# One extra load ahead of the position loads: 8 bytes from each of 111 stretches of the embedding table, read by every DMA engine

## The chip, the cores and the metric

The kernel runs on one core of one Trainium2 chip. The metric is device time in microseconds (us), the median of several executions. The text also uses the *span* of a profiled execution, from the first to the last instruction that the profile shows; in undisturbed runs here it is about 2 us shorter than the device time.

## The reference

```python
def setup_inputs():
    batch, seq_len, vocab_size, d_model = 32, 512, 50000, 512
    ...   # int32 indices, float32 table (50000 x 512), float32 positions (512 x 512)

def reference(indices, embedding_table, position_embed):
    token_embed = embedding_table[indices]
    return (token_embed + position_embed).astype(np.float32)
```

It looks up 16,384 rows of 2 KB each in a table of 102 MB, adds a position row to each, and writes 33.5 MB. The indices reach the chip as 64-bit integers.

## The kernel before

GpSimd issues 128 gathers. Each fetches 128 rows, one per partition (256 KB). VectorE adds the position rows, which ScalarE has copied to PSUM, and SyncE issues the stores: one per gather in the first two batches and the last, one per two gathers in five more, one per batch of four gathers (1 MB) in the rest. All small loads go out on SyncE's queue, in the order in which they are written.

```python
    idx0 = const.tile([P, 2 * K], i32)
    nc.sync.dma_start(out=idx0[:], in_=idx_first)               # indices of batch 0
    idx_raw = const.tile([B, S, 2], i32)
    nc.sync.dma_start(out=idx_raw[:], in_=idx_words.rearrange("b (s w) -> b s w", w=2))
    pos_sb = [const.tile([P, D], f32, name=f"pos_sb{k}") for k in range(K)]
    for k in range(K):
        nc.sync.dma_start(out=pos_sb[k][:], in_=pos_rows[:, k, :])
    ...                                                          # indices turned: idx_t
    pos_ps = [psum.tile([P, D], f32, name=f"pos_ps{k}") for k in range(K)]
    for k in range(K):
        nc.scalar.copy(out=pos_ps[k][:], in_=pos_sb[k][:])

    def chunk(b, parts):
        at = 0
        for n in parts:
            data = data_pool.tile([P, n, D], f32, tag="data")
            for j in range(n):
                k = at + j
                where = idx0[:, 2 * k : 2 * k + 1] if b == 0 else idx_t[:, k, b : b + 1]
                nc.gpsimd.indirect_dma_start(out=data[:, j, :], out_offset=None, in_=table,
                    in_offset=bass.IndirectOffsetOnAxis(ap=where, axis=0))
                nc.vector.tensor_tensor(out=data[:, j, :], in0=data[:, j, :],
                                        in1=pos_ps[k][:], op=add)
            nc.sync.dma_start(out=out_rows[b][:, at : at + n, :], in_=data[:])
            at += n
```

## Time and profile before

| | before |
|---|---|
| device time, median of 3 | 184.50 us (184.49 to 184.75) |
| the profiled execution | 177.94 us, span 176.2 us |
| moved by DMA | 68.33 MB |
| GpSimd, 128 gathers | 1.25 us from one to the next |

The profiled execution is 6.6 us shorter than the timed ones.

The first lines are from the page of the kernel before. "DMA" is the mean busy share, in tenths, of the core's 16 DMA engines in 40 equal slices of the span; "GB/s" is what they moved. The line with L88 is the group of gathers: busy time, mean ns of one, and the idle time before them. The last lines are DMA issues with the median us from issue to landing.

```profile
span 176.2 us, 480 instructions
DMA  4889999999999999999999999999999999999995
GB/s 131 305 236 354 384 380 387 414 410 406 417 378 397 413 413 407 402 404 390 419 419 415 415 421 412 415 413 414 419 420 416 415 408 421 406 399 406 413 411 205
...
DMA 57%; POOL 27%; issue 11%; DVE 2%; POOLq 0%; DVEq 0%
...
L88 POOL DMA_INDIRECT data<-in_embedding_table_dram,idx_t x124 | 117.2, 945 | 39.8 <-issue 33.7
...
data<-in_embedding_table_dram,idx_t POOLq DMA_INDIRECT x124, 7.7
pos_sb<-in_position_embed_dram SPq DMA_DIRECT2D x4, 256.0 KB, 4.7
```

From the seventh slice to the last but one the DMA engines move 378 to 421 GB/s and are busy throughout. In slices 2 and 3 (counted from 0; 9 to 18 us) they are busy too, and move less. That stretch is what the change was made for.

The timeline of GpSimd in the same trace shows the first gather, three in the middle, and the last. The columns are start, duration, engine, line, operation, and in brackets the idle time before.

```profile
2.94 1.14 POOL L88 DMA_INDIRECT data<-in_embedding_table_dram,idx  x1 [1.74 <-DMA idx<-in_indices_dram]
...
40.61 0.95 POOL L88 DMA_INDIRECT data<-in_embedding_table_dram,idx_t  x1 [0.30 <-issue]
41.86 0.95 POOL L88 DMA_INDIRECT data<-in_embedding_table_dram,idx_t  x1 [0.30 <-issue]
43.11 0.95 POOL L88 DMA_INDIRECT data<-in_embedding_table_dram,idx_t  x1 [0.30 <-issue]
...
163.88 0.95 POOL L88 DMA_INDIRECT data<-in_embedding_table_dram,idx_t  x1 [0.30 <-DVE data L94]
```

GpSimd takes one step of 1.25 us per gather. Had it kept that step from the first gather (2.94, which is followed by one gap of 1.44) to the end, the last gather would start at 2.94 + 1.44 + 126 x 1.25 = 161.9 us. It starts at 163.9. 256 KB per 1.25 us is 210 GB/s of reads and, in time, as much of writes. So GpSimd asks for 420 GB/s, and the DMA engines deliver 414 over the 60 us from 100 us on.

### The profile page before, as it was taken

To read this page: it belongs to the slowest core of one execution; us is meant where nothing else is said; L and a number is where in the kernel's file an instruction comes from. 1 tells how busy PE (TensorE), PEld (TensorE's weight loads), DVE (VectorE), ACT (ScalarE), POOL (GpSimd) and SP (SyncE) were. 2 spreads that over 40 slices of the span, in tenths; PEclk is the share of its full clock that TensorE was granted. 3 is DMA by queue.
4 is the path that set the end of the run, shared out by engine and by line. 5 is a ranking of instruction groups with operands and counts; after the bars stand their busy time and mean duration, and the time that the engine had idled before them with its cause. 6 is when DMAs were issued, how large, how long until landed. Compare 5 with 4: busy or idle time off the path is not lost.

```text
span 176.2 us, 480 instructions
## 1 busy us (share of the span) xinstructions
PE 0.7 (0%) x4; PEld 0.6 (0%) x4; DVE 87.7 (50%) x130; ACT 3.6 (2%) x5; POOL 121.7 (69%) x134
## 2 busy tenths in 40 slices
PE   0100000000000000000000000000000000000000
PEld 0100000000000000000000000000000000000000
DVE  1162554454744447354466464544647464444740
ACT  2410000000000000000000000000000000000000
POOL 3777777777777777777777777777777756777300
DMA  4889999999999999999999999999999999999995
GB/s 131 305 236 354 384 380 387 414 410 406 417 378 397 413 413 407 402 404 390 419 419 415 415 421 412 415 413 414 419 420 416 415 408 421 406 399 406 413 411 205
DMA packets 17635, 68.33 MB, mean 388 GB/s; under 512 B 3008, under 2 KB 3008, under 8 KB 14560
## 3 DMA queue, kind: packets, MB, share of 16 engines
q0 software_dynamic: 10240, 33.56, 50.2%
q1 hardware_dynamic: 7392, 34.74, 48.1%
q14 instruction: 3, 0.02, 0.0%
HBM read 34.74 MB, written 33.55 MB: 388 GB/s over the span
## 4 chain that ended last, share of the span: by engine, by line
DMA 57%; POOL 27%; issue 11%; DVE 2%; POOLq 0%; DVEq 0%
DMA data<-in_embedding_table_dram,idx_t 56%; POOL data L88 27%; DVE data L94 2%; DMA idx<-in_indices_dram 1%; POOLq L88 0%; DVEq L94 0%
## 5 line engine op out<-in xcount | busy, mean ns | idle before, releaser
L88 POOL DMA_INDIRECT data<-in_embedding_table_dram,idx_t x124 | 117.2, 945 | 39.8 <-issue 33.7
L94 DVE TENSOR_TENSOR data<-data,pos_ps 128x512 f32<-128x512 f32 x128 | 86.9, 687 | 79.6 <-DMA data<-in_embedding_table_dram,idx_t 72.7
L88 POOL DMA_INDIRECT data<-in_embedding_table_dram,idx x4 | 4.0, 993 | 2.7 <-DMA idx<-in_indices_dram 1.7
L79 ACT COPY pos_ps<-pos_sb 128x512 f32<-128x512 f32 x4 | 2.4, 589 | 4.9 <-DMA pos_sb<-in_position_embed_dram 4.8
L68 DVE CAST idx_f<-idx_raw 32x512 f32<-32x512 int32 x1 | 0.5, 523 | 3.8 <-DMA idx_raw<-in_indices_dram 3.8
L79 ACT ACT_TABLE_LOAD x1 | 1.3, 1283 | 0.8 <-PEq L121 0.8
L75 DVE CAST idx_t<-turned 128x128 int32<-128x128 f32 x1 | 0.3, 292 | 0.8 <-PE turned L73 0.8
L73 PE MATMUL turned<-ident,idx_f 32*128 32x32 f32 x4 | 0.7, 300 | 4.4 <-DVE idx_f L68 4.4
L73 PEld LDWEIGHTS turned<-ident,idx_f 32*128 32x128 f32 x4 | 0.6, 206 | 4.4 <-issue 4.4
L121 POOL MEMSET const-float32-0.0<- 128x1 f32 x1 | 0.1, 105 | 0.3 <-issue 0.3
L60 POOL MEMSET ones<- 32x32 f32 x1 | 0.1, 114 | 0.3 <-POOLq L121 0.3
L62 POOL TENSOR_SCALAR_AFFINE_SELECT ident<-ones 32x32 f32<-32x32 f32 x1 | 0.2, 202 | 0.1
L121 POOL MEMSET const-uint8-127<- 128x1 uint8 x1 | 0.1, 122 | 0.0
L121 POOL MEMSET const-bfloat16-1.0<- 128x1 bf16 x1 | 0.1, 116 | 0.0
L121 POOL MEMSET const-float32-1.0<- 128x1 f32 x1 | 0.1, 108 | 0.0
## 6 DMA issues: line engine op xcount, KB each, us to landing
out_dram<-data SPq DMA_DIRECT2D x24, 1024.0 KB, 7.7
out_dram<-data SPq DMA_DIRECT2D x10, 512.0 KB, 6.9
out_dram<-data SPq DMA_DIRECT2D x12, 256.0 KB, 5.8
data<-in_embedding_table_dram,idx_t POOLq DMA_INDIRECT x124, 7.7
pos_sb<-in_position_embed_dram SPq DMA_DIRECT2D x4, 256.0 KB, 4.7
idx_raw<-in_indices_dram SPq DMA_DIRECT2D x1, 128.0 KB, 2.5
data<-in_embedding_table_dram,idx POOLq DMA_INDIRECT x4, 4.7
idx<-in_indices_dram SPq DMA_DIRECT2D x1, 4.0 KB, 1.8
```

Source lines behind the costliest of these rows:

```text
L60: nc.gpsimd.memset(ones[:], 1.0)
L62: nc.gpsimd.affine_select(out=ident[:], in_=ones[:], pattern=[[-1, B]], compare_op=mybir.AluOpType.is_equal, fill=0.0, base=0, channel_mul ...
L68: nc.vector.tensor_copy(out=idx_f[:].rearrange("b p k -> b (p k)"), in_=idx_raw[:, :, 0])
L73: nc.tensor.transpose(turned[:, k, :], idx_f[:, :, k], ident[:])
L75: nc.vector.tensor_copy(out=idx_t[:], in_=turned[:])
L79: nc.scalar.copy(out=pos_ps[k][:], in_=pos_sb[k][:])
L88: nc.gpsimd.indirect_dma_start(out=data[:, j, :], out_offset=None, in_=table, in_offset=bass.IndirectOffsetOnAxis(ap=where, axis=0),)
L94: nc.vector.tensor_tensor(out=data[:, j, :], in0=data[:, j, :], in1=pos_ps[k][:], op=add)
L121: nc = _bacc.Bacc("TRN2", target_bir_lowering=False, num_devices=1)
```

## The change

The idea is that an engine's first read in some part of the table may be slow, and that 8 bytes read early from each part take that slowness out of the gathers. The load is third in SyncE's queue: behind the indices, which the gathers need at once, and ahead of the position rows.

```diff
+STRETCHES = 112
...
     nc.sync.dma_start(
         out=idx_raw[:], in_=idx_words.rearrange("b (s w) -> b s w", w=2)
+    )
+
+    step = -(-V // STRETCHES)
+    touched = const.tile([16, V // step, 2], f32)
+    nc.sync.dma_start(
+        out=touched[:],
+        in_=bass.AP(table.tensor, 0, [[0, 16], [step * D, V // step], [1, 2]]),
     )
     pos_sb = [const.tile([P, D], f32, name=f"pos_sb{k}") for k in range(K)]
```

`step` is 447 rows (0.92 MB), so there are 111 reads per engine. Nothing reads `touched`.

## The prediction

> **What bounds the kernel now.** The 16 DMA engines. From slice 6 of 40 on, the page's DMA row reads 9 tenths and the GB/s row 380 to 420; the kernel moves 68.33 MB, which at 415 GB/s alone takes 165 of the 176.2 us span. GpSimd issues one gather of 256 KB per 1.25 us, 210 GB/s of reads and as much of writes: 420 together, just what the DMA carries. So a backlog made early is never worked off: the issue loop alone would start the last gather at 161.7 us; it starts at 163.9 and lands 7.3 us later.
>
> **Where it loses time.** The GB/s row begins 131 305 236 354 384 380. From 9 to 18 us the engines are busy (8 tenths and more) and move little. The DMA records show why: a gather packet of 4096 B takes 159 ns in the steady state, but 230 to 440 ns on average from 9 to 13 us, single ones over 1000. Summed over the run, gather packets lose 6.0 us per engine against 159 ns, about half of it in the first 24 of 128 gathers. By 26.4 us 7.9 MB are moved; at 415 GB/s from the first store (9.3 us) it would be 9.3 MB. So 3 to 3.5 us are lost at the start. I take it that an engine's first reads in a part of the table are slow. This is a hypothesis: the trace doesn't name the cause, nor did I find it in the Trainium skill. Rival: the first writes to the output (the bad stretch starts with the first store).
>
> **What the change adds.** One load on the SP ring, behind both index loads and before the four position loads; the order on GpSimd, DVE and ACT stays. The partition dimension is 16, so by the Trainium skill, "DMA: Bandwidth & Descriptors", section "Why a DMA increments its semaphore by 16", all 16 engines take part, each with 111 reads of 8 B, one per 0.9 MB. Packets of 4 to 32 B took 7 to 9 ns here: 1 us per engine if the reads are quick; I estimate 1.5 to 4 us with the slow first reads inside. The first gather keeps its start. The position loads (last one in at 8.1 us) come 1.5 to 3 us later, and with them first add (8.54) and first store (9.26). In that time the engines only carry 210 GB/s of gathers, so half of the delay is lost: 0.7 to 1.5 us.
>
> **Sum.** -3.5 us if all early slowness goes, +0.7 to 1.5 for late stores, perhaps -0.5 from rarer long packets at 40 to 90 us, and a fair chance that the touch does nothing: about -2.7. GpSimd's cadence caps the gain near 6 us.
>
> Predicted: 181.8 us, 8 times in 10 within 178.2 to 185.3. Faster by over 2%: 0.33; within 2%: 0.58; slower: 0.09.
>
> **What would show it.** Right: gather packets near 159 ns from 9 to 20 us, slices 2 to 4 at 380 or more, the 2.1 us GpSimd stall at 144 us gone, last gather issued near 162 us, gather landings below 7.7 us. First add at 10 to 11.5 us. Wrong: the same long packets at 9 to 18 us (then it is the output, or parts smaller than 0.9 MB), or a touch that takes over 5 us.
>
> **What would make it wrong.** Descriptor generation for 1776 pieces may be slow on SP and hold up the position loads; slow first reads may serialise in the touch, moving the cost instead of hiding it; or the timed runs, 6.6 us longer than the profiled one, may be colder, and the gain larger.

## The result

| | before | after |
|---|---|---|
| device time, median of 4 | 184.61 us (184.49 to 184.75) | 184.51 us (184.49 to 184.56) |
| ratio | | 0.9995, 95% interval 0.9978 to 1.0012 |

A ratio is the mean time of one kernel's fast runs over that of the other's fast runs of the same rounds, so it is not quite the ratio of the medians. By this measure the change does nothing. The lines of the page of the changed kernel that answer to those of before:

```profile
span 182.8 us, 482 instructions
DMA  5999999999999999999999999999999999999910
GB/s 61 329 331 353 382 395 356 417 389 408 413 399 404 399 411 411 406 414 418 413 411 414 411 405 421 402 419 413 412 414 412 413 407 424 395 419 419 391 40 0
...
issue 63%; POOL 18%; DMA 7%; SPq 4%; DVE 1%; DVEq 0%
...
data<-in_embedding_table_dram,idx_t POOLq DMA_INDIRECT x124
pos_sb<-in_position_embed_dram SPq DMA_DIRECT2D x4, 256.0 KB
```

Three things are to be seen.

First, the last two slices are empty (40 and 0 GB/s): the last DMA packet ends at 174.5 us, against 174.7 us in the trace of before, but the span goes on to 182.8 us.

Second, the last column of the issue lines (us to landing) is missing, and the chain reads "issue 63%". Most semaphore records of this trace are missing: the semaphore with 112 recorded DMA updates in the trace of before has 30 in this one. So the chain and the named waits of this page can't be used. Engine times and DMA packets can.

Third, what fills the end is SyncE. These are the semaphore waits of the last line of each kernel, with minimum, median and maximum duration in ns, then first and last start; the kernel before is first, the changed kernel second.

```profile
L132 SPq EVENT_SEMAPHORE  x12: 17/28/28, 172.3 to 176.2; - x12
```

```profile
L140 SPq EVENT_SEMAPHORE  x12: 2/12/699, 176.3 to 182.7; - x12
```

In the trace of before, the closing waits that had nothing left to wait for follow each other at 0.06 us. In the changed kernel's trace SyncE starts a new instruction only every 0.70 or 1.40 us from 170.7 to 181.9 us, waits and store issues alike; nine of them start after the last packet:

```
start us  duration ns   (SyncE in the changed kernel's trace, some lines left out)
169.989   332   store
170.708   710   wait
172.109   710   store
...
178.407    12   wait
179.108     2   wait
179.807     2   wait
```

This end is 8.3 us from last packet to end of span, against 1.5 us in the trace of before; with the last packet 0.2 us earlier, that is the 6.6 us by which the two spans differ, and 184.5 exceeds 177.9. All timed runs of *both* kernels in this first set took 184.5 to 184.8 us, so it seems to belong to the set rather than to the change. No trace of the kernel before shows it. I call it the slow end. The experiments had to ask that first, and then why the change gives nothing with or without it.

### The profile page after: what moved, and what is told of

Same layout as the page of the kernel before. It is cut to its first block, busy times and chain, and to the rows that moved or that the text cites. A ratio compares the mean times of both kernels' runs of the same rounds, so it can differ in the third digit from the quotient of the medians.

```text
span 182.8 us, 482 instructions
## 1 busy us (share of the span) xinstructions
PE 0.7 (0%) x4; PEld 0.6 (0%) x4; DVE 87.7 (48%) x130; ACT 3.6 (2%) x5; POOL 121.8 (67%) x134
## 2 busy tenths in 40 slices
DMA packets 19427, 68.34 MB, mean 374 GB/s; under 512 B 4800, under 2 KB 4800, under 8 KB 16352
## 4 chain that ended last, share of the span: by engine, by line
issue 63%; POOL 18%; DMA 7%; SPq 4%; DVE 1%; DVEq 0%
POOL data L96 18%; SPq L105 4%; DMA data<-in_embedding_table_dram,idx_t 4%; DMA out_dram<-data 3%; DMA idx<-in_indices_dram 1%; DVE data L102 1%; DVEq L102 0%
```

## The experiments

The theory of the prediction (T1): first reads in a part of the table are slow, 3 to 3.5 us of DMA time are lost to them at the start, and lost DMA time is never made up. Rival T2: the slowness belongs to the first writes to the output. Rival T3, formed after the first runs: GpSimd's issue sets the pace and the DMA engines, which have room, follow it; a long gather packet marks an engine with little queued, not lost time.

There is no run e11 on record. Eleven of the twelve runs were on one chip and e13 on another, each with the kernel before beside it, which took 177.9 to 178.1 us on both. None showed the slow end. So they can be compared with each other, and not with the 184.5 us above. All are correct except the narrow rows. The table is read from the traces. "MB by" sums the DMA packets of 512 bytes and more that ended by that time. "Over 400 ns" counts gather packets of 4096 bytes that took longer than that, in all of the 8192, and of those that started between 16 and 60 us.

| run | ratio to before | first gather | first add | MB by 10 us | by 20 | by 40 | by 160 | over 400 ns, all | 16-60 us |
|---|---|---|---|---|---|---|---|---|---|
| first trace of before | | 2.94 | 8.54 | 2.16 | 5.36 | 13.29 | 62.46 | 114 | 40 |
| first trace of the change | (0.9995) | 2.67 | 8.22 | 2.06 | 5.43 | 13.28 | 62.46 | 77 | 51 |
| e1 before again | 0.9998 | 2.68 | 8.24 | 2.22 | 5.54 | 13.32 | 62.63 | 99 | 47 |
| e2 change again | 1.0039 | 2.72 | 7.78 | 2.06 | 5.51 | 13.32 | 61.92 | 114 | 43 |
| e3 446 stretches | 1.0081 | 2.68 | 13.60 | 0.46 | 4.26 | 12.38 | 61.98 | 66 | 0 |
| e4 narrow rows | 1.0002 | 2.97 | 9.35 | 2.15 | 5.35 | 13.27 | 62.35 | 92 | 39 |
| e5 446 in one place | 1.0296 | 2.74 | 21.31 | 0.29 | 2.62 | 10.58 | 60.44 | 99 | 2 |
| e7 load after positions | 1.0031 | 2.67 | 9.26 | 1.77 | 5.25 | 13.20 | 62.21 | 96 | 30 |
| e8 111 in one place | 1.0009 | 2.75 | 10.75 | 1.11 | 4.90 | 13.16 | 62.42 | 17 | 13 |
| e10 late gathers | 1.0212 | 6.33 | 10.03 | 1.45 | 4.33 | 11.83 | 61.12 | 131 | 66 |
| e12 change, third | 1.0032 | 2.67 | 8.07 | 2.10 | 5.49 | 13.21 | 62.42 | 64 | 37 |
| e13 late adds | 1.0015 | 2.67 | 13.10 | 2.20 | 4.81 | 12.98 | 62.57 | 81 | 23 |

### Does the slow end belong to the change? (e1, e2)

e1 is the kernel before, e2 the changed kernel, both unedited.

> The kernel before, unchanged, to see which of two things its profile shows. Its timed runs took 184.5 us, its one profile 176.2 us of span, while the changed kernel's profile has 182.8 us of span with the last DMA packet at 174.5 us and then about 8 us in which SyncE takes 0.70 us over each instruction. Theory A (the slow end belongs to every timed run of either kernel, and the first profile of before was the exception): this profile now shows a span of about 182.8 us, last packet near 174.7, and SyncE instructions 0.70 us apart at the end. Theory B (the slow end is a cost of the extra load): span 176.2 again, last SyncE waits 0.06 us apart, and the 184.5 us of the timed runs comes from somewhere outside the span.

> The changed kernel, unchanged, as a second look at it on the same chip as the run above. Theory A: ratio 1.00 within 0.3%, span 182.8 us, SyncE 0.70 us per instruction from about 170 us on. Theory B: the same span for this kernel but not for before. Early part by either: GB/s of slices 1 to 3 near 330, 330, 355; gather packets lose about 5.4 us per engine over the run.

Measured: before 178.1 us against 178.1 (ratio 0.9998, 0.9968 to 1.0029), the change 179.1 us (1.0039, 1.0001 to 1.0076). Neither shows the slow end. The same line as above, for the kernel before in e1 and then for the changed kernel in e2:

```profile
L132 SPq EVENT_SEMAPHORE  x12: 17/28/28, 172.1 to 175.9; - x12
```

```profile
L140 SPq EVENT_SEMAPHORE  x12: 17/28/28, 174.3 to 177.9; - x12
```

Both theories as I had written them fail. The slow end belongs neither to every timed run of a kernel (A) nor to the extra load (B): it came with the first set of runs and stayed away in the four later ones. What caused it stays open, since it did not come back and can't be called up; which chip the first set ran on is not on record, so the chip is not ruled out. It came in a trace that lacked most semaphore records, so it may have to do with the recording; that is a guess.

Without it, the change is no gain. It is a third of a per cent slower.

### Is it where in the table one reads? (e3, e4)

e3 reads four times as densely; e4 makes the gathers read only the first 3.2 MB of the table.

```diff
 e3, against the change
-STRETCHES = 112
+STRETCHES = 448
 e4, against the kernel before (wrong on purpose)
-    nc.vector.tensor_copy(out=idx_f..., in_=idx_raw[:, :, 0])
+    nc.vector.tensor_scalar(out=idx_f..., in0=idx_raw[:, :, 0], scalar1=1.0 / 32, op0=mult)
     ...                       # and the same for idx0
```

> As the change, with 448 stretches instead of 112 (446 reads of 8 bytes per engine, one per 0.23 MB). If slow first reads belong to parts of the table smaller than 0.9 MB, the long gather packets go away for the most part: loss below 2.5 us per engine and last packet about 2 us earlier than 174.5. If they have nothing to do with where in the table one reads, they stay near 5 us, and the load only costs: position loads and first add about 3 us later, last packet 1 to 2 us later. In the timed ratio the slow end may hide either.

> The kernel before, wrong on purpose: each index is divided by 32 on the chip, so that all gathers read the first 3.2 MB of the table; one or two small VectorE operations more. If the slow stretch at 9 to 18 us comes from first reads across 102 MB of table, the long gather packets go away (loss of gather packets well below 2 us, slices 2 and 3 at 350 or more instead of 236 and 354) and the last packet comes 2 to 4 us earlier. If it comes from the first writes to the output, both stay as before: about 6 us lost, 236 GB/s in slice 2.

The two seem to contradict each other. This is the GB/s row of the page, e3 first, then e4:

```profile
GB/s 36 65 297 387 403 379 409 417 417 418 416 422 418 411 417 412 408 413 412 415 422 417 421 402 413 408 419 417 416 423 405 424 410 422 411 385 416 417 404 195
```

```profile
GB/s 125 291 269 340 385 407 386 397 398 411 416 382 389 401 414 413 388 408 411 409 416 417 406 406 415 411 416 413 418 415 412 419 408 409 419 408 416 415 408 159
```

With 446 stretches, no gather packet that starts between 16 and 60 us is over 400 ns, which looks like T1. But with gathers that read only 3.2 MB of the table, the long packets stay (92 against 99 in e1), the rates of slices 2 and 3 stay low (269 and 340), and the time is the same (1.0002). If first reads across 102 MB were slow, e4 would have lost that slowness. By the measure set beforehand, e3 speaks against T1 as well: summed over the run, gather packets lose 5.6 us per engine against 159 ns each, where below 2.5 was asked for (e1: 5.5), because they are long while the load runs; and the last packet comes at 175.9 us, not 2 us before 174.5. T2 has a difficulty too: in e3 the first store comes at 14.3 us, and the stretch after it is not slow.

The traces of the change itself point the same way. They have 51, 43 and 37 gather packets over 400 ns between 16 and 60 us, the kernel before 40 and 47; from 9 to 18 us the mean gather packet takes 202 to 205 ns, in the kernel before 241 and 219. The change hardly did what it was made for.

What e3 also does is hold the position rows back, so that the first add comes at 13.6 us. Meanwhile the gathers pile up. That was the alternative to test.

### Tiny reads that visit nothing (e5, e8)

Same count and size of reads as in e3 and in the change, but within a few KB at the start of the table.

```diff
-        in_=bass.AP(table.tensor, 0, [[0, 16], [step * D, V // step], [1, 2]]),
+        in_=bass.AP(table.tensor, 0, [[0, 16], [4, V // step], [1, 2]]),
```

> 446 reads of 8 bytes per engine as in the dense touch, but all within the first 7 KB of the table, so the load takes ring time and holds up the position loads and warms nothing else. If the dense touch removed the long gather packets by visiting the whole table, they come back here after the load ends: loss of gather packets after the first 16 gathers above 1.5 us (1.9 us in the kernel before from gather 12 on, 0.7 in the dense touch). If they went away because the delay leaves a longer queue of gathers on each engine, they stay away: no packet over 400 ns after 12 us. Time 1.003 to 1.010 of before.

> The change with the same 111 reads of 8 bytes per engine, all within the first 2 KB of the table. If spreading the reads over the table is worth anything, this is slower than the change (above 1.004); if the spread itself costs (slow first reads in the load), it is faster (near 1.001 to 1.002), and the load lands clearly sooner than the change's position loads did: first position copy before 6.0 us. If only the ring time matters, it equals the change at 1.004.

Here is the GB/s row of e8:

```profile
GB/s 31 134 388 371 394 415 410 415 413 415 421 384 402 414 415 413 409 407 409 407 414 416 413 412 413 409 409 413 418 412 417 408 416 408 409 412 415 418 406 183
```

This is the profile that the prediction asked for: slices 2 to 4 near 380, and only 17 gather packets over 400 ns instead of 99. The load that brings it about visits 2 KB of the table. So the long packets go away without any other part of the table having been read before, and T1 falls. (The load did not land sooner, as one of the expectations had it, but later: 7.0 us against 3.7, with the first position copy at 9.24 us.) The time does not fall with the packets: ratio 1.0009 (0.9986 to 1.0032). By 10 us e8 is 1.1 MB behind e1, by 40 us 0.16 MB, and by 160 us 0.2 MB. Of 2.7 us of DMA work (1.1 MB at 410 GB/s) almost all is made up, and beyond that nothing is gained. e8 does change two things at once, shorter packets and later position rows, and a gain from the one could hide a cost of the other. By the prediction's own terms that would be an estimated 0.8 us of gain: 2.0 us for gather packets, which lose 3.5 us per engine instead of 5.5, less half of the 2.5 us by which the first add is later. Measured was +0.2 us (-0.2 to +0.6), so the terms do not hold together; no run has the short packets without the late start.

e5 missed its expected time (1.0296 instead of 1.003 to 1.010), because its load took 14.3 us to land, against 9.0 us for the same 446 reads spread over the table. For 111 reads it was 7.0 against 3.7 us. It too has hardly any long packets after 16 us (2). Its first add is 13 us late, and it costs 5 us: more than can be made up, but far from all of it. e3, with its first add 5.4 us late, costs 1.4 us; the section on late gathers comes back to both.

### Where in the queue? (e7)

```diff
+    for k in range(K):
+        nc.sync.dma_start(out=pos_sb[k][:], in_=pos_rows[:, k, :])
     step = -(-V // STRETCHES)
     ...                                    # the extra load
-    for k in range(K):
-        nc.sync.dma_start(out=pos_sb[k][:], in_=pos_rows[:, k, :])
```

> The change with its load behind the position loads instead of ahead of them. If what the change costs (ratio 1.004 on the second chip) is the later position loads, this is at 1.000 to 1.002 of before; if it is the ring time of 111 tiny reads per engine or the slow reads themselves, it stays near 1.004. If touching helps at all once nothing waits for it, the ratio is below 0.998.

Measured: 1.0031 (1.0005 to 1.0057), much as in e2. The third of a per cent does not go away when the position rows no longer wait behind the load. That does not rule the wait out as its cause in e2, for e7 brings a delay of its own: moved behind them, the load took 8.0 us to land, the median landing of the first four gathers rose from 4.6 us (e1) to 6.4, and the first add came at 9.26 us.

### Late adds and stores, without any extra load (e6, e9, e13)

The prediction charged half of any delay of the first store. To test that alone, ScalarE is kept busy ahead of the position copies. Two attempts failed to make the delay: the program's scheduler put the real copies in among the idle ones (e6), or held back one of four position buffers only (e9). e13 makes it.

```diff
 e6: 18 copies into a tile of their own      (reordered, first add still at 8.3 us)
 e9: 18 copies into pos_ps[0]                (adds of one slot in four held back)
 e13:
+    idle = const.tile([P, D], f32)
+    nc.vector.memset(idle[:], 0.0)
+    for _ in range(5):
+        for k in range(K):
+            nc.scalar.copy(out=pos_ps[k][:], in_=idle[:])
     for k in range(K):
         nc.scalar.copy(out=pos_ps[k][:], in_=pos_sb[k][:])
```

> The kernel before, with 18 ScalarE copies of 0.59 us ahead of the position copies, so that the first add and the first store come at about 13.6 us as in the dense touch, and no load is added. It tells what long packets belong to. If they come from first reads in the table, they appear from 6 to 13 us while gathers run alone. If they come with the first stores, none appear before 13.6 us and some after. If they only mark an engine with a short queue, they appear while gathers run alone (210 GB/s offered to engines that can do 415), and are few afterwards, when gathers and a pile of stores keep the queue long. Last packet 1 to 2 us later than before, ratio 1.005 to 1.012.

> The delay that the earlier run with ScalarE copies failed to make: 18 copies into the first position buffer itself, so the first add waits for them until about 13.5 us; no load is added, the gathers are untouched. If a store that is late by 5 us is lost time on the DMA engines, as the prediction had it (half of the delay), the kernel takes 2 to 3 us more, ratio 1.012 to 1.017. If the kernel is bound by how fast GpSimd issues gathers until about 40 us and the DMA engines have slack there, the delay is made up: MB moved at 40 us within 0.3 of the 13.35 of before, ratio below 1.006. Long gather packets: if they need only a short queue, none over 400 ns after about 15 us; if tiny reads are what removes them, they stay as before.

> Third form of the delay by ScalarE, now with five idle copies into each of the four position buffers, so that no add can start before about 13 us (8.2 us in the kernel before); no load is added and the gathers start as before. Prediction's term (half of a delay of the stores is lost): 5 us late, so 2.5 us more, ratio 1.014. If the DMA engines have slack up to about 40 us and GpSimd sets the pace: ratio below 1.004, MB moved at 15 us about 0.8 lower and at 40 us within 0.3 of 13.35. Gather packets over 400 ns: few between 15 and 40 us if a longer queue is what removes them (as after the 446 reads of one place), as many as before (some 25) if the tiny reads did it.

e6 measured 1.0008 (0.998 to 1.0036) and e9 1.0005 (0.9988 to 1.0022); as they made little or no delay, they say little. e13 measured 1.0015 (0.999 to 1.0041) with the first add at 13.10 us instead of 8.24. Almost 5 us late costs 0.3 us, with an interval that includes no cost at all, where the prediction's rule says 2.5 (or an estimated 1.6 if the shorter gather packets, which lose 4.7 us per engine instead of 5.5, are credited in full). How it is made up is seen by stages (e1 and e13 are on different chips). The columns are the stretch and its length, busy time (and number of instructions) of PE, PEld, DVE, ACT and POOL, the clock, the DMA share and GB/s. First the kernel before (e1), then e13:

```profile
9.00:14.00 5.00, 0.00 (x0) 0.00 (x0) 2.71 (x4) 0.01 (x1) 3.78 (x4) 1.00 0.90 270
14.00:20.00 6.00, 0.00 (x0) 0.00 (x0) 2.36 (x4) 0.00 (x0) 4.60 (x5) 1.00 1.02 373
20.00:26.00 6.00, 0.00 (x0) 0.00 (x0) 3.25 (x6) 0.00 (x0) 4.48 (x6) 1.00 1.01 362
26.00:40.00 14.00, 0.00 (x0) 0.00 (x0) 7.40 (x12) 0.00 (x0) 10.65 (x12) 1.00 1.01 401
40.00:60.00 20.00, 0.00 (x0) 0.00 (x0) 11.16 (x17) 0.00 (x0) 15.13 (x17) 1.00 1.01 404
```

```profile
9.00:14.00 5.00, 0.00 (x0) 0.00 (x0) 0.90 (x2) 5.00 (x10) 3.78 (x4) 1.00 0.78 232
14.00:20.00 6.00, 0.00 (x0) 0.00 (x0) 4.57 (x8) 0.63 (x2) 4.65 (x5) 1.00 0.94 290
20.00:26.00 6.00, 0.00 (x0) 0.00 (x0) 3.02 (x5) 0.00 (x0) 4.48 (x6) 1.00 1.04 399
26.00:40.00 14.00, 0.00 (x0) 0.00 (x0) 7.30 (x11) 0.00 (x0) 10.65 (x12) 1.00 1.02 414
40.00:60.00 20.00, 0.00 (x0) 0.00 (x0) 11.18 (x17) 0.00 (x0) 15.12 (x17) 1.00 1.01 409
```

GpSimd's column is the same in both. e13 moves less up to 20 us and more from then on: 399, 414 and 409 GB/s where the kernel before runs at 362, 401 and 404. So between 20 and 60 us the engines carry more with a pile of work in front of them than they do in the kernel before, although the DMA share reads 1.01 and more. The DMA share says that the engines had a packet open; it does not say that they were at their limit.

The long packets go in the same direction. In the first trace of before, 12% of the gather packets that started with one or two gathers outstanding (issue finished, packets not yet started) took over 200 ns; with two to three it was 3.0%, with three to four 1.4%, with four to five 0.4%. This alone is a correlation, and the 12% are mostly the start of the run: of the packets that started after 16 us it was 1.6, 2.4, 1.4 and 0.4%. But e3, e5 and e8, which pile up gathers early, all show few long packets afterwards, wherever they read. e13, with a pile of adds and stores instead, has half as many as e1 between 16 and 60 us (23 against 47): not the "few" that I expected. Of its gather packets, 36 over 400 ns started before its first store (13.81 us), which speaks against T2.

### Late gathers (e10)

Sixteen small VectorE copies stand between the first index load and the first gather.

```diff
+    for n in range(16):
+        later = const.tile([P, 2 * K], i32, name=f"later{n}")
+        nc.vector.tensor_copy(out=later[:], in_=idx0[:])
+        idx0 = later
     idx_raw = const.tile([B, S, 2], i32)
```

> The kernel before with 16 small VectorE copies between the first index load and the first gather, so that GpSimd starts about 2 to 2.5 us later and all else can start as before. If GpSimd's issue sets the pace up to 40 us, this delay, unlike that of the stores, is not made up early: MB at 40 us lower by 0.6 to 1.0 (2.3 us at 420 GB/s), ratio 1.006 to 1.014. If the early part has slack for any delay, the ratio stays below 1.004.

The delay came out at 3.65 us instead of 2 to 2.5. The first and last gather in the timeline of GpSimd, for e10 and then for the kernel before (e1):

```profile
6.33 1.14 POOL L92 DMA_INDIRECT data<-in_embedding_table_dram,later  x1 [5.13 <-DVE idx_t L79]
...
166.54 0.95 POOL L92 DMA_INDIRECT data<-in_embedding_table_dram,idx_t  x1 [0.30 <-issue]
```

```profile
2.68 1.14 POOL L88 DMA_INDIRECT data<-in_embedding_table_dram,idx  x1 [1.48 <-DMA idx<-in_indices_dram]
...
163.21 0.95 POOL L88 DMA_INDIRECT data<-in_embedding_table_dram,idx_t  x1 [0.30 <-DVE data L94]
```

The ratio is 1.0212 (1.0186 to 1.0237), which is 3.8 us. A late first gather is passed on in full; 1.5 MB are missing at 40 us and still at 160 us. Set beside e13 and e8: delay the stores by 5 us and 0.3 us remain; delay the position rows by a load so that 1.1 MB are missing at 10 us, and 0.2 us remain; delay GpSimd's gathers by 3.65 us and 3.8 us remain. This fits T3, but does not prove it. All that the kernel moves after the small loads hangs on a gather, so a late first gather would be passed on if the DMA engines set the pace too. What e8 and e13 show is that a small backlog of the DMA engines is made up.

e3 and e5 show where that ends. e3 is 1.28 MB behind e1 at 20 us and still 0.65 at 160; e5 is 2.9 and 2.2 MB behind. Their first gathers start as in e1 (2.68 and 2.74 us). Their last ones, e3 first, do not:

```profile
165.01 0.95 POOL L96 DMA_INDIRECT data<-in_embedding_table_dram,idx_t  x1 [0.30 <-DVE data L102]
```

```profile
167.37 0.95 POOL L96 DMA_INDIRECT data<-in_embedding_table_dram,idx_t  x1 [0.30 <-issue]
```

What GpSimd's steps take beyond 1.25 us adds up to 1.8 us in e1, 3.4 in e3 and 5.8 in e5. So a backlog that is large enough does reach GpSimd, and neither side alone sets the pace. It does not follow that a faster GpSimd would gain much: from 100 to 160 us the engines move 415 GB/s in e1 and in e13 alike, so there they seem close to their own limit. No run tried it.

### How much does the change cost? (e12)

The changed kernel once more, unedited, five rounds.

> The changed kernel for the third time, five rounds, to settle whether it costs a third of a per cent: 1.0039 on the second chip with an interval from 1.0001. Expected 1.002 to 1.005 and SyncE waits 0.06 us apart at the end. Should this chip show the slow end (SyncE 0.70 us per instruction), both kernels take 184.5 us and the ratio is 1.000.

Measured: 178.47 us, 1.0032 (1.0017 to 1.0048). So the cost is real and about 0.6 us. Its cause stays open. e7 did not remove it, and e8, with as many reads in one place, is at 1.0009, with an interval that overlaps. In the trace of e2 the loss comes late, between 60 and 100 us, where it moves 399 GB/s against 411 in e1; the trace of e12 has no such stretch. The profiled runs of e2 and e7 were the slowest of theirs (179.6 and 179.4 us); in their traces what GpSimd's steps take beyond 1.25 us adds up to 3.5 and 3.4 us, in that of e12 (178.2 us) to 1.3.

No experiment pointed to a kernel that beats the one before. What they point to, an earlier first gather or a shorter step per gather, was not to be had by an edit of this kernel: the first gather already waits only for its 4 KB of indices, and one gather instruction with four indices per partition, as I tried it, did not build (no run shows this).

## Why the prediction was wrong

It gave 181.8 us, 1.5% faster; measured was no change in the first set (0.9995) and 0.3 to 0.4% slower in the two others. The time lies in the range stated, but only because the range was wide. It also gave "a fair chance that the touch does nothing", and that is what came. Two steps failed: that the long packets are first reads in the table, on which the 3.5 us of gain rested, and that a backlog made early is never worked off, by which lost DMA time became lost time of the kernel.

- **"What bounds the kernel now. The 16 DMA engines."** This is one half of the truth. The same paragraph had the other number: GpSimd asks for 420 GB/s, "just what the DMA carries". I took the DMA side because it was 9 tenths busy and had a backlog. e13 shows that the engines, up to about 60 us, have room for stores that are 5 us late, at a cost of 0.3 us; e10, that 3.65 us of late gathers cost 3.8. That GpSimd's issue sets the pace fits both and is not shown by itself; e3 and e5 show that a large backlog holds GpSimd up.
- **"So a backlog made early is never worked off."** This step failed. e8 makes up almost all of 1.1 MB by 40 us. e13 is 0.7 MB behind e1 at 20 us, 0.3 at 40, and 0.06 at 160. It is wrong for small backlogs only: of 1.28 MB in e3 half was left at 160 us (0.65), and it cost 1.4 us.
- **"So 3 to 3.5 us are lost at the start."** The largest term of the sum. The change gained none of it, as it left the long packets; e8, which takes nearly all of them away, gained nothing either and moves no more MB by 40 us, but starts 1.1 MB behind. The term compared 7.9 MB at 26.4 us with the 9.3 that 415 GB/s would have moved. By then about 9.05 MB had been asked for: the small loads, 18 gathers issued by GpSimd, and the stores of 12. So 1.2 MB were outstanding, not lost. In e13 1.96 MB were outstanding at that time, with 7.35 moved, and it takes about 0.3 us more than the kernel before.
- **"An engine's first reads in a part of the table are slow."** This is the step on which the gain rested, and it failed. It is refuted twice: the long packets stay when the gathers read only 3.2 MB (e4, 92 over 400 ns against 99), and go when the tiny reads visit only 2 KB (e8, 17). The change itself left 51, 43 and 37 of them between 16 and 60 us in its three traces, against 40 and 47 before. The rival named in the prediction, the first writes to the output, is not borne out either: in e3 and e8 the stretch that follows the first store has almost none, and in e13 36 came before it. That they go with little queued fits e3, e5 and e8, but is not shown apart from the early start of the run; what such a packet waits for, no record names.
- **"The position loads ... come 1.5 to 3 us later, and with them first add (8.54) and first store (9.26)", "half of the delay is lost".** The first position copy starts 1.5 us later in the first trace of the change (6.04 against 4.55), but the last, which frees the fourth add, only 0.45 us later (9.17 against 8.72). The first add is no later at all (7.8 to 8.2 us in the three traces of the change). The rule of half the delay is wrong as well: e13 lost 0.3 us of 4.9.
- **The signs it named.** Right: the last gather was issued near 162 us in the first trace (162.3), but in e2 at 165.2, so this varies. Wrong: slices 2 to 4 read 331, 353 and 382 where 380 or more was asked, and the first add did not come at 10 to 11.5 us. The wait of GpSimd at 144 us (2.1 us before) was 0.7 us, but it also varies from run to run: 1.8 us in e1 and 1.7 us in e2. Gather landings took 7.8 us in e2 and e12, where less than 7.7 was asked.
- **"16 engines take part, each with 111 reads."** Right. The Trainium skill, "DMA: Bandwidth & Descriptors", section "Why a DMA increments its semaphore by 16 and not by 1", has all 16 engines take part where the slowest dimension of both sides is 16, as it is here. The page counts 19,427 packets against 17,635, 1,792 more, which is 16 x 111 reads and 16 completions. The estimate of 1.5 to 4 us for the load holds (3.7 us from issue to landing in e2).
- **The timed runs.** The prediction saw that they were 6.6 us longer than the profiled one and guessed that they might be "colder". In the one such trace that there is, it was the slow end of SyncE, behind the last packet.

## What to carry to other kernels

Where two limits lie within a few per cent of each other, ask which one a delay passes through: hold back one side alone by a few us (the issuing engine, then the consumers) and see which delay reaches the end. Mind what hangs on the side that is held back: a late first gather delays all that follows it, so the delay of the consumers tells more. Use more than one size of delay, too; a small one can be made up where a large one is not. A busy DMA row and slow packets are no proof of a DMA limit; count the bytes that had been asked for by that time, and those outstanding, and compare kernels by the MB moved at a few fixed times. When a timed run and a profile differ by several us, look at what follows the last packet before explaining anything else by it.

## What the Trainium skill lacked or had wrong

- **"DMA: Bandwidth & Descriptors", section "Where 436 GB/s comes from".** It gives 435 GB/s as the ceiling of the ports. This mix of 2 KB rows read and 8 KB rows written moves 414 to 415 GB/s over the 60 us from 100 us on in the kernel before. A gather packet of 4096 bytes takes 159 ns, a store packet of 8192 bytes 309 ns; with 16 engines that makes 412 and 424 GB/s, on either side of what was measured.
- **No page has it: reads of 8 bytes by all engines take longer when they go to one place.** 446 per engine landed after 14.3 us within 7 KB of the table, and after 9.0 us when spread over 102 MB; 111 per engine after 7.0 and 3.7 us. The median record of such a packet reads 9 ns in all four, so it does not show it.
- **No page has it: gather packets are longer at the start, when little is queued.** Over 200 ns were 12% of them with one or two gathers outstanding and 0.4% with four to five, in the first trace of before; after 16 us it was 1.6 and 0.4%, so early and little queued are not told apart. The busy share of the DMA engines counts this as work.
- **No page has it: SyncE at 0.70 us per instruction from about 170 us on, and most semaphore records missing, in the first set of runs.** The times of both kernels were 6.6 us longer there; only the trace of the changed kernel shows how. It was absent from all twelve runs after. Its cause is open.
